# Keys scaled by one VectorE operation a head, probabilities scaled on GpSimd by a per-row scalar and in two portions

## The chip, the cores and the metric

The kernel runs on one core of one Trainium2 chip. The core has a matrix engine (TensorE, PE in the profile, with its weight loads listed apart as PEld), a vector engine (VectorE, DVE), an activation engine (ScalarE, ACT), a general engine (GpSimd, POOL) and a queue that issues transfers (SyncE, SP). Each engine takes its instructions in a fixed order and waits at an instruction until what it needs is there. The metric is the device time of one execution in microseconds (us); lower is better.

## What is computed

The reference is a trunk of two layers over 528 tokens (16 learned "meta" tokens ahead of 512 tokens) with 1024 channels. A layer normalises the stream, projects it, runs a causal pooling mixer and a latent attention side by side, gates both and adds the result to the stream. The change touches the attention alone, whose core is this:

```python
k = jnp.concatenate([k_nope, k_pe], axis=-1)      # 64 own columns a head, 32 rotary columns shared by all heads
q = rmsnorm(q, g_qn)
k = rmsnorm(k, g_kn)                              # one factor for each token and head
q = jnp.concatenate([q[..., :64], apply_rope(q[..., 64:], pos)], axis=-1)
k = jnp.concatenate([k[..., :64], apply_rope(k[..., 64:], pos)], axis=-1)
s = jnp.einsum('bqhd,bkhd->bhqk', q, k) * scale   # by blocks of 128 queries, causal
p = jax.nn.softmax(s, axis=-1)
o = jnp.einsum('bhqk,bkhd->bqhd', p, v)
```

There are 8 heads. The softmax divides each row of exponentials by its sum; the normalisation of the keys multiplies each key by a factor of its token and head.

## The kernel before

Channels lie on the 128 partitions and tokens along the free dimension. Each product in single precision is made of three matrix products (`mm3`, lines 187 to 193): a weight tile of 128 by 512 is loaded into `raw`, ScalarE rounds it to `whi` (line 183) and VectorE computes the rest `wlo = raw - whi` (line 184). Both inputs of that subtraction lie in SBUF. A stream of such products (`stream`, line 204) is the main work; the attention is threaded through it. In the program, `gap()` lets a set length of the stream run (2950 ns and 2700 ns a gap in layers 0 and 1, `FILL`), so that a head's parts stand between stretches of products. The order that each engine finally follows is set when the program is built: it is made with `schedule_with_timeline_sim=True`, so a scheduler lays the instructions out along a simulated timeline, and an instruction that stands later in the program may go ahead of one that is not ready there.

Heads go in pairs. The tile `kn[p]` holds the 64 own key rows of head 2p in partitions 0 to 63 and those of head 2p+1 in partitions 64 to 127. The tile `kp` holds the rotated shared key rows in both halves. For each head, `prep(h)` (line 842) builds the scaled keys `kf` (a buffer named `tmp`): VectorE multiplies the 64 own rows by the factors `bc` (line 849) and GpSimd multiplies the 64 shared rows by the same factors (line 850). `bc` is fetched two heads ahead by `spread_k` (line 838). Then `split` rounds `kf` to `kh` on ScalarE and takes the rest `kl` on VectorE (lines 297 and 298), the query of the head is split into `qhl`, and two transfers on the SP queue bring the rotary rows of the query (line 860).

`head(h)` (line 863) has two halves. In the first it computes the scores of query blocks 1 and 2 and part of block 3, takes the row minima on VectorE (`top`, line 879; it writes `bia`) and the exponentials of blocks 1 and 2 on ScalarE (`expo`, line 886, which also writes the row sums `rs`). A gap and the value products of the head before (`pv(prev, (0, 1))`) follow, and a second gap. In the second half come the rest of block 3, block 0 and their exponentials, the addition of the two partial sums of block 3 (line 918), one reciprocal of all four sums (line 919), and then GpSimd scales all four blocks. For each block it runs two multiplications of two tensors, one for the 16 meta columns, written to the pair's tile `pm` (line 924), and one for the other columns in place (line 926); in both the second tensor is the reciprocal spread along the row. The blocks `pt[0]` and `pt[1]` lie in `pa`, `pt[2]` and `pt[3]` in slots named `cq`. The number of columns is 144, 272, 400 and 528.

`pv` (line 929) of the next head transposes the scaled blocks on TensorE, splits the transposes (`th`, `tl`) and multiplies them with the values; for an odd head it splits `pm` (lines 939 to 941).

GpSimd also issues transfers that add weight tiles in memory for a later stage (`wsum`, `wsumgp`, line 353). Layer 1 has more vector work among the heads than layer 0: `mixed` (line 579) and the products made of seven instead of eight parts (`fast`, line 601, with lines 625 to 651).

Of the kernel before, what the change touches and what calls it, by code (L numbers as in the profile page):

```python
# [9 lines left out]
F32 = mybir.dt.float32  # L10
# [4 lines left out]
ALU = mybir.AluOpType  # L15
# [3 lines left out]
P = 128  # L19
# [3 lines left out]
NM = 16  # L23
# [49 lines left out]
def trunk(ctx, tc, xT, pos, win, wkr, wqb, wkb, wvb, wgr, wpu, wmu, wout, gains, const, yT):  # L73
    nc = tc.nc
    pe, act, dve, gp, sp = nc.tensor, nc.scalar, nc.vector, nc.gpsimd, nc.sync
# [11 lines left out]
    def nm(s):  # L87
        uid[0] += 1
        return f"{s}_{uid[0]}"
# [269 lines left out]
    class Layer:  # L359
# [158 lines left out]
        def k_factors(self):  # L518
            flat = lambda d: d.rearrange("h (s c) -> (h s) c", c=T // 16)
            na, ny, nt = (sm.tile([P, T // 16], F32, tag=t, name=nm(t)) for t in ("ka", "ky", "kt"))  # L520
            sp.dma_start(na, flat(ksr[self.l]))
            dve.tensor_scalar(na, na, 1.0 / QK, EPS, op0=ALU.mult, op1=ALU.add)
            newton(ny, na, nt)
            sp.dma_start(flat(kdr[self.l]), ny)
            self.bcs = {}
            for h in range(2):
                self.spread_k(h)

        def rope(self, out, src, a, b):
            n = b - a  # L530
# [307 lines left out]
        def spread_k(self, h):  # L838
            self.bcs[h] = bc = slot("bc", bufs=3)
            sp.dma_start(bc, kdr[self.l][h:h + 1, :].partition_broadcast(P))  # L840

        def prep(self, h):
            p, odd = h // 2, h % 2
            n0, r0 = (64, 0) if odd else (0, 64)
            kf = tmp()
            bc = self.bcs.pop(h)
            if h + 2 < H:
                self.spread_k(h + 2)
            dve.tensor_mul(kf[n0:n0 + 64, :], self.kn[p][n0:n0 + 64, :], bc[n0:n0 + 64, :])
            gp.tensor_mul(kf[r0:r0 + 64, :], self.kp[r0:r0 + 64, :], bc[r0:r0 + 64, :])  # L850
            kh, kl = slot("kh", F32R, bufs=2), slot("kl", F32R, bufs=2)
            split(kh, kl, kf[:, :T], 0, T)
            qh, ql = qhl[odd]
            x0 = self.x0
            src = self.qn[p][n0:n0 + 64, x0:T]
            act.activation(qh[n0:n0 + 64, x0:T], src, AF.Copy)
            dve.tensor_sub(ql[n0:n0 + 64, x0:T], src, qh[n0:n0 + 64, x0:T].bitcast(F32))
            g0 = 32 * (h % 4)
            for d, f in zip((qh, ql), self.qr[h // 4]):
                sp.dma_start(d[r0:r0 + 32, x0:T].bitcast(F32), f[g0:g0 + 32, x0:T].bitcast(F32))  # L860
            return kh, kl, qh, ql

        def head(self, h, kq, prev, between):
            kh, kl, qh, ql = kq
            odd = h % 2
# [19 lines left out]
            def expo(i, c, sv, pv):  # L885
                act.activation(pv, sv, AF.Exp, scale=-1.0, bias=bia[:, i:i + 1], accum_out=rs[:, c:c + 1])  # L886

            pt = [pa[:, 0:144], pa[:, 144:416], pb[:, 0:400], pc[:, 0:T]]
            sa = sct()
            s1, s3 = sa[:, 0:272], sa[:, 272:272 + SPL]  # L890
# [10 lines left out]
            top(2, 2, s2, causal(400))  # L901
            expo(1, 1, s1, pt[1])
            expo(2, 2, s2, pt[2])
            self.gap()
            between()
            self.pv(prev, (0, 1))
# [9 lines left out]
            expo(3, 3, s4, pt[3][:, SPL:T])  # L916
            expo(0, 0, s0, pt[0])
            dve.tensor_add(rs[:, 3:4], rs[:, 3:4], rs[:, 4:5])
            dve.reciprocal(rs[:, 0:4], rs[:, 0:4])  # L919
            if odd == 0:  # L920
                self.pm = sm.tile([P, 4, 32], F32, tag="pm", name=nm("pm"), bufs=2)
            for i in range(4):
                n = pt[i].shape[1]
                gp.tensor_mul(self.pm[:, i, 16 * odd:16 * odd + 16], pt[i][:, 0:NM],  # L924
                              rs[:, i:i + 1].to_broadcast([P, NM]))
                gp.tensor_mul(pt[i][:, NM:], pt[i][:, NM:], rs[:, i:i + 1].to_broadcast([P, n - NM]))  # L926
            return h, pt, self.pm

        def pv(self, prev, js):
# [483 lines left out]
```

## Time and profile before

| what | us |
|---|---|
| median of 3 runs | 786.03 |
| lowest and highest run | 784.74, 787.63 |
| the profiled execution | 788.06 |
| its span, from the first to the last instruction | 786.2 |

The difference between the profiled execution and its span, 1.86 us, is time outside the first and last instruction. The page of the profile gives for each engine its busy time and its share of the span. The views used below are: busy times by stretch of the span, waits (who waited for whom: total us, number of times, longest), groups of instructions by line (count, busy us, mean ns of one, then idle time just before them and who ended it), durations of one line (minimum/median/maximum), and the timeline. The heads of layer 0 lie between 160 and 340 us, those of layer 1 between 590 and 700 us.

### The profile page before, as it was taken

The numbers are of one execution on the slowest core, as the hardware profiler recorded it, in microseconds if no ns is written. First come the engines' busy times: TensorE is split into PE (matmuls) and PEld (weight loads), VectorE is DVE, ScalarE is ACT, GpSimd is POOL, SyncE is SP. The second block draws the span as 40 slices with busy tenths as digits, with TensorE's granted clock in tenths as the row PEclk, the third lists the DMA queues.
The fourth block names the chain that finished last, engine by engine and source line by source line (L and its number), as shares of the span: only waits on it lengthen the run. The fifth ranks groups of instructions, "written<-read, shape, count | busy, mean of one in ns | idle before, by whom it ended". The sixth has DMA issues, their size and how long they took to land.

```text
span 786.2 us, 15369 instructions
## 1 busy us (share of the span) xinstructions
PE 774.8 (99%) x5469; PEld 711.1 (90%) x5469; DVE 587.0 (75%) x1316; ACT 446.7 (57%) x1022; POOL 230.2 (29%) x319
## 2 busy tenths in 40 slices
PE   9999999999999999999999999999999999999998
PEld 8999899999999999999997898887788899788887
DVE  5848788547778977689764477775997899974984
ACT  8545655645556665545664356455667676654462
POOL 1024514203434342211320245131026235240213
PEclk9999999999999999999999999999999999999999
DMA  6242367765645465565653423435456566562655
GB/s 243 82 97 87 103 163 165 180 154 136 144 120 138 120 135 150 135 187 155 172 151 92 102 81 95 125 88 181 121 132 162 160 168 164 150 212 88 213 148 136
DMA packets 64909, 110.76 MB, mean 141 GB/s; under 512 B 10544, under 2 KB 16560, under 8 KB 64832
## 3 DMA queue, kind: packets, MB, share of 16 engines
q1 hardware_dynamic: 54928, 90.02, 38.4%
q0 software_dynamic: 8896, 17.92, 12.6%
q10 hardware_dynamic: 1008, 1.84, 0.6%
q8 instruction: 43, 0.70, 0.4%
q14 instruction: 34, 0.28, 0.1%
HBM read 100.18 MB, written 22.62 MB: 156 GB/s over the span
## 4 chain that ended last, share of the span: by engine, by line
PE 84%; DVE 6%; DMA 4%; issue 2%; ACT 2%; POOL 0%; SPq 0%; DVEq 0%; ACTq 0%
PE mm L188 24%; PE mm L192 23%; PE mm L191 23%; DVE wlo L184 2%; PE S L188 2%; PE S L191 2%; PE S L192 2%; PE mm L946 2%; DMA raw<-wsumgp 1%; DMA raw<-win 1%; PE o L952 1%; PE o L951 1%; PE S L500 1%; ACT whi L183 1%; DMA raw<-wqb 1%
## 5 line engine op out<-in xcount | busy, mean ns | idle before, releaser
L188 PE MATMUL mm<-hh,whi 128*128 128x264 f32 (+2 forms) x992 | 306.0, 311 | 1.6 <-DVE tmp L637 0.6
L192 PE MATMUL mm<-hh,wlo 128*128 128x264 f32 (+2 forms) x992 | 304.1, 309 | 1.1 <-DVE wlo L184 1.0
L191 PE MATMUL mm<-hl,whi 128*128 128x264 f32 (+2 forms) x992 | 304.5, 308 | 0.0
L184 DVE TENSOR_TENSOR wlo<-raw,whi 128x512 fp32r<-128x512 f32 (+2 forms) x261 | 191.9, 739 | 98.1 <-ACT whi L183 94.3
L183 ACT ACTIVATE whi<-raw 128x512 fp32r<-128x512 f32 (+2 forms) x261 | 156.5, 603 | 165.9 <-PE mm L191 91.0
L188 PEld LDWEIGHTS mm<-hh,whi 128*128 128x128 f32 x992 | 186.2, 188 | 12.9 <-issue 1.2
L192 PEld LDWEIGHTS mm<-hh,wlo 128*128 128x128 f32 x992 | 185.8, 188 | 10.6 <-DVE wlo L184 2.3
L191 PEld LDWEIGHTS mm<-hl,whi 128*128 128x128 f32 x992 | 186.8, 188 | 9.1
L188 PE MATMUL mm<-cq,whi 128*128 128x264 f32 (+2 forms) x140 | 44.2, 316 | 1.3 <-ACT racc L960 0.7
L192 PE MATMUL mm<-cq,wlo 128*128 128x264 f32 (+2 forms) x140 | 43.5, 313 | 0.6 <-DVE wlo L184 0.6
L191 PE MATMUL mm<-cq,whi 128*128 128x264 f32 (+2 forms) x140 | 43.5, 312 | 0.0
L879 DVE CUSTOM_DVE_ANT_0 S<-S,maskw,nqs 128x288 f32<-128x288 f32 (+4 forms) x80 | 38.4, 497 | 2.5 <-PE S L192 2.2
L702 POOL TENSOR_TENSOR racc<-racc,tmp 128x264 f32<-128x264 f32 (+1 forms) x15 | 14.3, 951 | 87.2 <-ACT tmp L701 87.1
L188 PE MATMUL mm<-u,whi 128*128 128x264 f32 (+1 forms) x108 | 35.3, 327 | 0.1
L192 PE MATMUL mm<-u,wlo 128*128 128x264 f32 (+1 forms) x108 | 34.8, 322 | 0.0
L298 DVE TENSOR_TENSOR tl<-mm,th 128x512 fp32r<-128x512 f32 (+1 forms) x64 | 29.2, 481 | 7.4 <-ACT th L297 6.3
L850 POOL TENSOR_TENSOR tmp<-kp,bc 64x528 f32<-64x528 f32 x16 | 25.6, 1602 | 30.5 <-issue 15.4
L353 POOL DMA_DIRECT2D wsum<-wout x8 | 6.9, 859 | 89.0 <-PE mm L192 73.0
L924 POOL TENSOR_TENSOR pm<-pa,rs 128x16 f32<-128x16 f32 x32 | 11.0, 345 | 72.6 <-DVE rs L919 66.7
L926 POOL TENSOR_TENSOR cq<-cq,rs 128x384 f32<-128x384 f32 (+1 forms) x32 | 32.2, 1005 | 0.0
L886 ACT ACTIVATE cq<-S,bia 128x400 f32<-128x400 f32 (+2 forms) x48 | 24.6, 515 | 12.2 <-DVE bia L914 7.2
L297 ACT ACTIVATE th<-mm 128x512 fp32r<-128x512 f32 (+1 forms) x64 | 25.9, 432 | 8.4 <-PE mm L946 7.3
(333 smaller groups left out, 1722.0 us busy)
## 6 DMA issues: line engine op xcount, KB each, us to landing
raw<-win SPq DMA_DIRECT2D x139, 256.0 KB, 3.0
raw<-wout SPq DMA_DIRECT2D x22, 256.0 KB, 3.5
bc<-kdr SPq DMA_DIRECT2D x16, 264.0 KB, 4.2
wsum<-wout SPq DMA_DIRECT2D x16, 256.0 KB, 3.5
raw<-wpu SPq DMA_DIRECT2D x16, 256.0 KB, 3.1
wsumgp<-win SPq DMA_DIRECT2D x16, 256.0 KB, 3.3
raw<-wmu SPq DMA_DIRECT2D x16, 256.0 KB, 2.7
raw<-wsumgp SPq DMA_DIRECT2D x16, 256.0 KB, 3.8
```

The costliest lines, as they stand in the source:

```text
L183: act.activation(hi[:, :n], raw[:, :n], AF.Copy)
L184: dve.tensor_sub(lo[:, :n], raw[:, :n], hi[:, :n].bitcast(F32))
L188: first = pe.matmul(out, wh, xh, start=start, stop=False, skip_group_check=more)
L191: pe.matmul(out, wh, xl, start=False, stop=False, skip_group_check=more)
L192: newest[0] = pe.matmul(out, wl, xh, start=False, stop=stop, skip_group_check=more)
L297: act.activation(hi[:, a:b], src, AF.Copy)
L298: dve.tensor_sub(lo[:, a:b], src, hi[:, a:b].bitcast(F32))
L850: gp.tensor_mul(kf[r0:r0 + 64, :], self.kp[r0:r0 + 64, :], bc[r0:r0 + 64, :])
L879: dve.tensor_tensor_reduce(out=sv, in0=sv, in1=mask, scale=nqs[:, i, h:h + 1], scalar=3e38, op0=ALU.add, op1=ALU.min, accum_out=bia[:, c:c ...
L886: act.activation(pv, sv, AF.Exp, scale=-1.0, bias=bia[:, i:i + 1], accum_out=rs[:, c:c + 1])
L926: gp.tensor_mul(pt[i][:, NM:], pt[i][:, NM:], rs[:, i:i + 1].to_broadcast([P, n - NM]))
L946: pe.transpose(tr[:, P * (i - j):P * (i - j + 1)], pt[i][:, NM + P * j:NM + P * (j + 1)], ident)
```

## The change

The keys: the shared rows in the lower half of `kp` are overwritten with the own rows of the pair's even head by a transfer on the SP queue (`lend`), so that `kp` holds a complete unscaled key of the even head, own rows below and shared rows above. The even head's `kf` is then one VectorE multiplication of 128 partitions. After the even head's multiplication is issued, another transfer writes the shared rows over the even head's rows in `kn[p]`, which makes `kn[p]` the complete key of the odd head, own rows above; its `kf` is again one VectorE multiplication. The first `lend` of a layer is issued in `k_factors`, the others in `prep` of the odd heads. GpSimd no longer takes part in the keys.

The probabilities: GpSimd scales each whole block in place by one `tensor_scalar`, whose factor is one number a partition, and copies the 16 scaled meta columns to `pm`. The blocks 1 and 2 get a reciprocal of their own right after their exponentials, in the first half of the head, and are scaled there; blocks 0 and 3 stay in the second half.

```diff
@@ k_factors
             for h in range(2):
                 self.spread_k(h)
+            self.lend(0)
...
+        def lend(self, p):
+            sp.dma_start(self.kp[0:64, :], self.kn[p][0:64, :])
+
         def prep(self, h):
...
-            dve.tensor_mul(kf[n0:n0 + 64, :], self.kn[p][n0:n0 + 64, :], bc[n0:n0 + 64, :])
-            gp.tensor_mul(kf[r0:r0 + 64, :], self.kp[r0:r0 + 64, :], bc[r0:r0 + 64, :])
+            dve.tensor_mul(kf, self.kn[p] if odd else self.kp, bc)
+            if not odd:
+                sp.dma_start(self.kn[p][0:64, :], self.kp[64:128, :])
+            elif p < 3:
+                self.lend(p + 1)
@@ head
+            if odd == 0:
+                self.pm = sm.tile([P, 4, 32], F32, tag="pm", name=nm("pm"), bufs=2)
+
+            def scale(blocks):
+                for i in blocks:
+                    gp.tensor_scalar(pt[i], pt[i], rs[:, i:i + 1], None, op0=ALU.mult)
+                    gp.tensor_copy(self.pm[:, i, 16 * odd:16 * odd + 16], pt[i][:, 0:NM])
...
             expo(1, 1, s1, pt[1])
             expo(2, 2, s2, pt[2])
+            dve.reciprocal(rs[:, 1:3], rs[:, 1:3])
+            scale((1, 2))
             self.gap()
...
             dve.tensor_add(rs[:, 3:4], rs[:, 3:4], rs[:, 4:5])
-            dve.reciprocal(rs[:, 0:4], rs[:, 0:4])
-            if odd == 0:
-                self.pm = sm.tile([P, 4, 32], F32, tag="pm", name=nm("pm"), bufs=2)
-            for i in range(4):
-                n = pt[i].shape[1]
-                gp.tensor_mul(self.pm[:, i, 16 * odd:16 * odd + 16], pt[i][:, 0:NM],
-                              rs[:, i:i + 1].to_broadcast([P, NM]))
-                gp.tensor_mul(pt[i][:, NM:], pt[i][:, NM:], rs[:, i:i + 1].to_broadcast([P, n - NM]))
+            dve.reciprocal(rs[:, 0:4:3], rs[:, 0:4:3])
+            scale((0, 3))
```

## The prediction

> **What bounds the kernel now.** I began with the page's busy times and its chain of waits, then cut the span into stretches at the two head stages.
>
> ```profile
> PE 774.8 (99%) x5469; PEld 711.1 (90%) x5469; DVE 587.0 (75%) x1316; ACT 446.7 (57%) x1022; POOL 230.2 (29%) x319
> ...
> PE 84%; DVE 6%; DMA 4%; issue 2%; ACT 2%; POOL 0%; SPq 0%; DVEq 0%; ACTq 0%
> ```
>
> ```profile
> core 0: us, PE busy (x) PEld busy (x) DVE busy (x) ACT busy (x) POOL busy (x), PEclk, DMA share, GB/s
> ...
> 160.00:340.00 180.00, 179.82 (x1463) 177.74 (x1463) 133.10 (x338) 102.08 (x264) 59.11 (x88) 1.00 0.57 137
> ...
> 590.00:700.00 110.00, 106.77 (x718) 96.75 (x717) 98.58 (x231) 75.19 (x197) 49.85 (x76) 1.00 0.63 170
> ```
>
> TensorE sets the end: it holds 84% of the chain and runs 774.8 of 786.2 us. The change gives it no work and takes none from it, so it can act only on the time in which TensorE stands still in the head stages, or add to it. In layer 0's heads (160 to 340) TensorE stands for 180 - 179.82 = 0.18 us: nothing is to be won there. In layer 1's heads (590 to 700) it stands for 110 - 106.77 = 3.23 us, and there VectorE is busy for 98.58 of 110 us, 90%, against 74% in layer 0's. So all that can be gained in the heads is 3.2 us, and VectorE is the engine that could lose it. The waits of that stretch, of TensorE, VectorE and ScalarE, say who is late:
>
> ```profile
> PE mm L192 <- DVE wlo L184: 1.0, 2, 0.8
> PE mm L188 <- ACT racc L960: 0.7, 1, 0.7
> PE mm L188 <- DVE tmp L637: 0.6, 1, 0.6
> PE o L951 <- DVE tmp L967: 0.6, 1, 0.6
> ```
>
> ```profile
> DVE wlo L184 <- ACT whi L183: 5.6, 7, 2.2
> DVE rs L918 <- ACT cq L886: 1.8, 3, 1.1
> ```
>
> ```profile
> ACT pmr L939 <- POOL pm L924: 4.3, 3, 2.2
> ```
>
> TensorE waits mostly for a VectorE result. VectorE itself waits 5.6 us for ScalarE's rounded weights, and ScalarE is held 4.3 us by GpSimd's `pm`. GpSimd is never waited for by TensorE but slows the two engines ahead of it. How, the timeline shows at one place, with the durations of the two VectorE lines beside it:
>
> ```profile
> 667.97 1.50 POOL L926 TENSOR_TENSOR cq<-cq,rs 128x512 f32<-128x512 f32 x1
> ...
> 669.55 1.99 POOL L850 TENSOR_TENSOR tmp<-kp,bc 64x528 f32<-64x528 f32 x1
> ```
>
> ```profile
> 668.50 1.52 DVE L184 TENSOR_TENSOR wlo<-raw,whi 128x512 fp32r<-128x512 f32 x1
> ...
> 670.28 1.80 DVE L184 TENSOR_TENSOR wlo<-raw,whi 128x512 fp32r<-128x512 f32 x1
> ```
>
> ```profile
> L184 DVE TENSOR_TENSOR wlo<-raw,whi x261: 281/692/1816, 6.4 to 773.9; 128x512 fp32r<-128x512 f32 x117, 128x256 fp32r<-128x256 f32 x10, 128x128 fp32r<-128x128 f32 x4
> ...
> L849 DVE TENSOR_TENSOR tmp<-kn,bc x16: 668/705/1756, 156.0 to 676.0; 64x528 f32<-64x528 f32 x16
> ```
>
> A subtraction of two SBUF tensors has a median of 692 ns, but 1.52 and 1.80 us where a GpSimd multiplication runs.
>
> **The change part by part.** These are the rows of VectorE and GpSimd in layer 1's heads:
>
> ```profile
> L184 DVE TENSOR_TENSOR wlo<-raw,whi 128x512 fp32r<-128x512 f32 x39 | 33.1, 849 | 5.6 <-ACT whi L183 5.6
> L849 DVE TENSOR_TENSOR tmp<-kn,bc 64x528 f32<-64x528 f32 x6 | 6.1, 1014 | 0.1
> ...
> L298 DVE TENSOR_TENSOR kl<-tmp,kh 128x528 fp32r<-128x528 f32 x6 | 4.2, 699 | 0.1
> ```
>
> ```profile
> L850 POOL TENSOR_TENSOR tmp<-kp,bc 64x528 f32<-64x528 f32 x6 | 10.2, 1698 | 20.4 <-issue 12.3 <-DVE rs L918 6.5 <-DVE kl L298 1.5
> L926 POOL TENSOR_TENSOR cq<-cq,rs 128x512 f32<-128x512 f32 x8 | 8.8, 1094 | 0.0
> L926 POOL TENSOR_TENSOR cq<-cq,rs 128x384 f32<-128x384 f32 x8 | 7.2, 900 | 0.0
> L924 POOL TENSOR_TENSOR pm<-cq,rs 128x16 f32<-128x16 f32 x16 | 6.1, 378 | 0.0
> L924 POOL TENSOR_TENSOR pm<-pa,rs 128x16 f32<-128x16 f32 x16 | 6.0, 372 | 31.5 <-DVE rs L919 29.6 <-DVE tl L298 1.8
> L926 POOL TENSOR_TENSOR pa<-pa,rs 128x256 f32<-128x256 f32 x8 | 5.5, 689 | 0.0
> L926 POOL TENSOR_TENSOR pa<-pa,rs 128x128 f32<-128x128 f32 x8 | 3.5, 440 | 0.0
> ```
>
> *Keys.* VectorE's operation grows from 64 to 128 partitions with the same 528 columns. Line 298 works on 128 by 528 in 699 ns and line 849 has a median of 705 ns on 64 by 528, so the wider operation costs the same: nothing added. GpSimd loses 1.70 us a head, and ScalarE's rounding of the keys loses one of its two releasers.
>
> *Probabilities.* GpSimd now spends 8.8 + 7.2 + 5.5 + 3.5 + 6.1 + 6.0 = 37.1 us, 4.64 us a head, and with the keys 6.34. The trace has no operation with a per-row factor on GpSimd. The nearest rows from both sides are a copy, with one input, and an addition of two full tensors:
>
> ```profile
> L476 POOL COPY tmp<-tmp x4: 398/772/806, 72.1 to 467.4; 32x264 f32<-32x264 f32 x4
> ```
>
> ```profile
> L702 POOL TENSOR_TENSOR racc<-racc,tmp 128x512 f32<-128x512 f32 x5 | 6.4, 1289 | 59.8 <-ACT tmp L701 59.8
> ```
>
> By its minimum the copy takes 398/264 = 1.51 ns a column with its fixed part, the addition 1289/512 = 2.52. The four blocks have 144 + 272 + 400 + 528 = 1344 columns: 2.0 us a head at the lower end, 3.4 at the upper. The four meta copies have the shape of line 924 (372 to 378 ns each in company): 1.5 us as an upper end, and 4 x 0.2 = 0.8 by estimate if they no longer meet as much of VectorE. I take 2.0 + 0.8 = 2.8 us a head, since an operation with one tensor is nearest to the copy; the ends are 2.8 and 4.9. Of 6.34 us that removes 56%, at the other end 23%.
>
> *What that gives VectorE.* In layer 1's heads the 39 subtractions cost 33.1 - 39 x 0.692 = 6.1 us more than at their median, line 849's six 6.1 - 6 x 0.705 = 1.9: 8.0 us lost to GpSimd. In proportion 56% is 4.5 us, 23% is 1.8. ScalarE gets back up to the 4.3 us before line 939, because GpSimd ends earlier. By the Trainium skill (SBUF — State Buffer, "SBUF: two separate sides") GpSimd and a VectorE operation with two SBUF inputs share one pair of ports as an exclusive lock, and the one that comes second is blocked for the whole of the other's instruction. The 1.80 us beside a GpSimd operation of 1.99 agree with it. By that rule fewer and shorter GpSimd operations count twice, and the relief would be nearer 1 - 0.44 x 0.44 = 81% of 8.0, 6.5 us; what this would make of the time is the second rival.
>
> *The added reciprocal.*
>
> ```profile
> L919 DVE RECIPROCAL rs<-rs x16: 160/178/178, 191.2 to 693.2; 128x4 f32<-128x4 f32 x16
> ```
>
> ```profile
> L886 ACT ACTIVATE cq<-S,bia x22: 441/494/597, 589.6 to 691.3; 128x288 f32<-128x288 f32 x8, 128x400 f32<-128x400 f32 x7, 128x240 f32<-128x240 f32 x7
> L886 ACT ACTIVATION_READ_ACCUMULATOR cq<-S,bia x22: 190/198/208, 590.0 to 691.6; 128x1 f32 x22
> ```
>
> One more a head, 8 x 0.17 = 1.4 us in layer 1's heads. It is also a new wait: it needs both exponentials of the first half, and behind it on VectorE stand the weight subtractions and the splits of transposes that TensorE waits for. At least this wait costs nothing, if other work is laid ahead of it for long enough; at most it lasts as long as both exponentials and their sums, 0.60 + 0.49 + 2 x 0.20 = 1.5 us a head, 12 us in the stage. The nearest row is the same kind of wait at line 918, 1.8 us in 8 heads; I take 1.8.
>
> *Transfers.* Per layer 4 `lend` and 4 back, on SP, of 64 x 528 x 4 bytes = 132 KB. The nearest rows are the query's transfers, also SBUF to SBUF, and what SP waits for between 550 and 700:
>
> ```profile
> qhl<-q SPq DMA_DIRECT2D x16, 66.0 KB, 2.9
> ```
>
> ```profile
> 658.50 1.16 SPq L860 DMA_DIRECT2D qhl<-q x2
> ```
>
> ```profile
> SPq L115 <- DVE wlo L184: 30.0, 19, 3.9
> ...
> SPq L840 <- POOL tmp L850: 2.8, 1, 2.8
> ```
>
> Each takes SP about 0.58 us to issue and some 3 to 4 us to land, and is needed a head later (110/8 = 14 us). Everything that it waits for was done a head earlier, so it holds up the weight loads behind it only by its issue, 8 x 0.58 = 4.6 us a stage, in a queue that waits 30.0 us for buffers anyway; the 2.8 us in which SP waited for line 850 go. I cost it at nothing. With that cover gone it would be 0.6 us a transfer on the way of a weight load, 4.6 us.
>
> *The sum in layer 1's heads.* VectorE: -4.5 + 1.4 + 1.8 = -1.3 us; ScalarE: up to -4.3 us of waiting. VectorE stays 88% busy, so some stalls remain; of TensorE's 3.23 us I give back half, 1.6, and nothing in layer 0's. Of the profiled execution's 788.06 us that leaves 786.5. It lies 2.03 us above the median of the runs, 786.03, so on their scale the forecast is **784.5 us**. Its own range is 783 to 786.
>
> **The rivals.** *The per-row factor is no cheaper* than a second tensor on GpSimd (4.9 us a head): VectorE gets 1.8 us and pays 1.4 + 1.8. Nothing changes, 786.0. For it: no row shows the operation. Against: the copy's 398 ns.
>
> *All the stalls go*: 786.03 - 3.2 = 782.8. For it: the 1.80 us beside 1.99 show a subtraction held for most of a GpSimd operation, so that shorter ones cost less than in proportion, and ScalarE's 4.3 us. The rule of the Trainium skill above speaks for it with its 6.5 us. Against: the chain through this stage also holds a late weight load, which no shorter operation mends:
>
> ```profile
> 660.38 4.96 DMA raw<-wsumgp
> ```
>
> *The new wait decides; slower.* Place: the reciprocal in the first half of a head of layer 1. VectorE's idle time there is 110 - 98.58 = 11.4 us, of which 5.6 is waiting for weights that can't be shifted; with the 4.5 gained and 1.4 spent, 8.9 us are free, 1.1 us a head. From there on each us of waiting is TensorE's. At 1.5 us a head it is (1.5 - 1.1) x 8 = 3.1 us: 789.1. If a rounding of weights (0.63 us in the row below) stands between the exponentials, 2.1 us a head and 8 us: 794. I take 790.5.
>
> ```profile
> L183 ACT ACTIVATE whi<-raw 128x512 fp32r<-128x512 f32 x40 | 25.2, 630 | 19.6 <-PE o L952 3.6 <-PE mm L946 3.5 <-PE mm L191 3.3
> ```
>
> For it: VectorE at 90%, and the changed lengths also let the planner lay out all engines anew, which can put this wait anywhere. Against: line 918 waits for the same thing and loses 1.8 us in 8 heads.
>
> **How the numbers follow.** Forecast 45%, no cheaper 15%, all stalls go 15%, slower 25%. About 0.5% (3.9 us) is what a measurement of this kernel can tell from no change: 782.1 to 790.0. Faster than that is a part of "all stalls go" and of luck in the layout, 12%. Slower is most of the slower case, 19%; the rest, 69%, is the same. The range goes from 781.8, all stalls and 1 us of spread between runs, to 790.8, the slower case with its lower half.
>
> **What would show it.** Right: GpSimd's time in layer 1's heads falls from 49.9 us to about 21; the mean of line 184 falls from 849 to below 770 ns; the wait of line 939 for GpSimd is gone; TensorE's 3.2 us of standing still shrink. Wrong: `tensor_scalar` rows above 2.5 ns a column; a wait of VectorE for line 886 in front of the new reciprocal of over 9 us in the stage; SP or a key split waiting for a `lend`; TensorE standing still in layer 0's heads, which would mean that the new layout, not the operations, decides.

## The result, and the profile after

The median of 7 runs of the changed kernel is **781.8 us** (780.91 to 783.88), against 786.03 before (now of 7 runs as well, with the same lowest, middle and highest): a ratio of 0.9951 with a 95% interval of 0.9939 to 0.9962, some 4.2 us or 0.5% less. The profiled execution took 781.06 us with a span of 779.3. The two profiled executions are 7.0 us apart, because the one of before lay 2.0 us above its median and this one 0.7 below; where a size matters, the medians decide.

The page of the changed kernel, busy times and the chain of waits by engine:

```profile
PE 772.7 (99%) x5469; PEld 711.3 (91%) x5469; DVE 570.4 (73%) x1332; ACT 445.9 (57%) x1022; POOL 232.1 (30%) x303
...
PE 90%; DMA 4%; DVE 3%; ACT 2%; issue 1%; POOL 1%; SPq 0%; ACTq 0%; DVEq 0%
```

TensorE runs the same 5469 matmuls and now holds 90% of the chain instead of 84%. Over the whole span it stood for 786.2 - 774.8 = 11.4 us before and stands for 779.3 - 772.7 = 6.6 now. GpSimd is *not* relieved: 232.1 us against 230.2, in 16 instructions fewer.

The stretches of the two head stages (busy us and instruction count of PE, PEld, DVE, ACT, POOL, then granted clock, DMA share, GB/s):

```profile
160.00:340.00 180.00, 180.00 (x1464) 177.90 (x1464) 126.66 (x347) 101.99 (x263) 58.93 (x80) 1.00 0.58 141
...
590.00:700.00 110.00, 109.55 (x736) 100.23 (x735) 92.06 (x240) 75.24 (x197) 54.95 (x69) 1.00 0.67 181
```

In layer 1's heads TensorE stands for 110 - 109.55 = 0.45 us instead of 3.23. VectorE is busy for 92.06 us instead of 98.58, although it has taken over GpSimd's key work; GpSimd is busy for 54.95 instead of 49.85.

VectorE's weight subtraction in that stretch (count, busy us, mean ns, then idle time before it and who ended it), and the new key operation in the whole run (minimum/median/maximum ns):

```profile
L184 DVE TENSOR_TENSOR wlo<-raw,whi 128x512 fp32r<-128x512 f32 x42 | 29.1, 695 | 10.0 <-ACT whi L183 9.5
```

```profile
L853 DVE TENSOR_TENSOR tmp<-kp,bc x8: 687/700/870, 155.0 to 662.8; 128x528 f32<-128x528 f32 x8
L853 DVE TENSOR_TENSOR tmp<-kn,bc x8: 689/698/703, 184.9 to 670.4; 128x528 f32<-128x528 f32 x8
```

The mean of line 184 has fallen from 849 to 695 ns, close to its median of before (692): hardly anything stretches it any more, and the longest one in this stretch takes 1.00 us instead of 1.80. The key operation over 128 partitions takes what the one over 64 took.

GpSimd in the same stretch, and below it the durations of its scaling in the whole run:

```profile
L900 POOL TENSOR_SCALAR cq<-cq,rs 128x528 f32<-128x528 f32 x8 | 14.9, 1864 | 0.0
L900 POOL TENSOR_SCALAR cq<-cq,rs 128x400 f32<-128x400 f32 x8 | 11.3, 1415 | 0.0
L900 POOL TENSOR_SCALAR pa<-pa,rs 128x144 f32<-128x144 f32 x8 | 8.2, 1023 | 9.5 <-DVE rs L936 5.1 <-ACT th L297 4.4
L900 POOL TENSOR_SCALAR pa<-pa,rs 128x272 f32<-128x272 f32 x7 | 8.1, 1161 | 28.9 <-DVE rs L919 28.9
L901 POOL COPY pm<-pa 128x16 f32<-128x16 f32 x16 | 6.4, 402 | 0.0
L901 POOL COPY pm<-cq 128x16 f32<-128x16 f32 x16 | 5.7, 359 | 0.0
```

```profile
L900 POOL TENSOR_SCALAR pa<-pa,rs x32: 632/960/2813, 180.7 to 689.4; 128x272 f32<-128x272 f32 x16, 128x144 f32<-128x144 f32 x16
L900 POOL TENSOR_SCALAR cq<-cq,rs x32: 1273/1597/2267, 181.7 to 690.3; 128x400 f32<-128x400 f32 x16, 128x528 f32<-128x528 f32 x16
```

A head's scaling (these six rows) takes 54.6/8 = 6.8 us of GpSimd, more than keys and probabilities together before (6.34). The shortest row, 632 ns for 144 columns, is 4.4 ns a column.

Waits between 580 and 700 us (total, times, longest):

```profile
DVE wlo L184 <- ACT whi L183: 10.5, 13, 2.3
...
ACT pmr L950 <- POOL pm L901: 0.4, 1, 0.4
```

ScalarE's 4.3 us of waiting for `pm` have become 0.4, and its waits for GpSimd's keys (1.6 us in two places before) are gone with that work. VectorE now waits 10.5 us for ScalarE's weights, not 5.6: it is ahead more of the time.

### The profile page after: what moved, and what is told of

The parts are those of the page before. It is cut to its first block, busy times and chain, and to the rows that moved or that the text cites. A ratio compares the mean times of both kernels' runs of the same rounds, so it can differ in the third digit from the quotient of the medians.

```text
span 779.3 us, 15360 instructions
## 1 busy us (share of the span) xinstructions
PE 772.7 (99%) x5469; PEld 711.3 (91%) x5469; DVE 570.4 (73%) x1332; ACT 445.9 (57%) x1022; POOL 232.1 (30%) x303
## 4 chain that ended last, share of the span: by engine, by line
PE 90%; DMA 4%; DVE 3%; ACT 2%; issue 1%; POOL 1%; SPq 0%; ACTq 0%; DVEq 0%
PE mm L188 26%; PE mm L192 25%; PE mm L191 25%; DMA raw<-win 2%; PE S L191 2%; PE S L192 2%; PE S L188 2%; PE mm L957 2%; PE o L963 1%; PE o L962 1%; PE S L500 1%; DVE wlo L184 1%; ACT whi L183 1%; DMA raw<-wqb 1%; PE mm L402 1%
## 5 line engine op out<-in xcount | busy, mean ns | idle before, releaser
L184 DVE TENSOR_TENSOR wlo<-raw,whi 128x512 fp32r<-128x512 f32 (+2 forms) x261 | 182.5, 703 | 104.6 <-ACT whi L183 100.5
L900 POOL TENSOR_SCALAR pa<-pa,rs 128x272 f32<-128x272 f32 (+1 forms) x32 | 33.2, 1036 | 103.3 <-DVE rs L919 63.9
L900 POOL TENSOR_SCALAR cq<-cq,rs 128x400 f32<-128x400 f32 (+1 forms) x32 | 51.1, 1597 | 0.0
L886 DVE CUSTOM_DVE_ANT_0 S<-S,maskw,nqs 128x272 f32<-128x272 f32 (+4 forms) x80 | 38.6, 498 | 5.3 <-PE S L192 5.0
L297 ACT ACTIVATE th<-mm 128x512 fp32r<-128x512 f32 (+1 forms) x64 | 26.2, 433 | 10.3 <-PE mm L957 9.8
L191 PE MATMUL mm<-kn,whi 128*128 128x264 f32 (+1 forms) x96 | 30.6, 320 | 0.0
```

What stands on the lines that cost most here:

```text
L184: dve.tensor_sub(lo[:, :n], raw[:, :n], hi[:, :n].bitcast(F32))
L191: pe.matmul(out, wh, xl, start=False, stop=False, skip_group_check=more)
L297: act.activation(hi[:, a:b], src, AF.Copy)
L886: dve.tensor_tensor_reduce(out=sv, in0=sv, in1=mask, scale=nqs[:, i, h:h + 1], scalar=3e38, op0=ALU.add, op1=ALU.min, accum_out=bia[:, c:c ...
L900: gp.tensor_scalar(pt[i], pt[i], rs[:, i:i + 1], None, op0=ALU.mult)
```

## The experiments

Two theories of where the 4.2 us come from. **Contention**: VectorE runs shorter, since fewer GpSimd instructions read two tensors. **Waiting**: what ScalarE and TensorE need no longer stands in GpSimd's queue. The change has three parts: *keys* (two transfers a pair, one VectorE multiplication a head), *form* (one `tensor_scalar` and a copy in place of two multiplications a block) and *move* (blocks 1 and 2 and their reciprocal in the first half). All eight combinations were timed, then single costs. Each time of a variant is the median of 8 to 12 runs, each ratio is against the kernel before on the same chip (785.82 to 786.35 us), with an interval of about 1 us on either side, so that two variants differ clearly from some 1.5 us on.

| version | median us | ratio (95%) | L184 mean ns, 590 to 700 | TensorE standing there, us | GpSimd busy there, us |
|---|---|---|---|---|---|
| before | 786.03 | 1 | 849 | 3.23 | 49.85 |
| keys | 784.18 | 0.9982 (0.9970 to 0.9994) | 778 | 1.71 | 43.03 |
| form | 788.52 | 1.0033 (1.0019 to 1.0047) | 727 | 1.55 | 58.90 |
| move | 789.27 | 1.0038 (1.0022 to 1.0053) | 811 | 4.62 | 50.62 |
| keys, form | 783.31 | 0.9974 (0.9963 to 0.9985) | 707 | 0.95 | 56.33 |
| keys, move | 784.37 | 0.9982 (0.9970 to 0.9994) | 762 | 1.26 | 40.62 |
| form, move | 786.31 | 0.9998 (0.9990 to 1.0007) | 780 | 2.01 | 64.76 |
| keys, form, move | 781.80 | 0.9951 (0.9939 to 0.9962) | 695 | 0.45 | 54.95 |

### One part alone

**keys_alone**, the kernel before with

```diff
+            self.lend(0)
...
+        def lend(self, p):
+            sp.dma_start(self.kp[0:64, :], self.kn[p][0:64, :])
...
-            dve.tensor_mul(kf[n0:n0 + 64, :], self.kn[p][n0:n0 + 64, :], bc[n0:n0 + 64, :])
-            gp.tensor_mul(kf[r0:r0 + 64, :], self.kp[r0:r0 + 64, :], bc[r0:r0 + 64, :])
+            dve.tensor_mul(kf, self.kn[p] if odd else self.kp, bc)
+            if not odd:
+                sp.dma_start(self.kn[p][0:64, :], self.kp[64:128, :])
+            elif p < 3:
+                self.lend(p + 1)
```

> Only the keys change (one VectorE multiplication of 128 partitions, the transfers between kp and kn); the scaling of the probabilities is that of before. Contention (GpSimd operations with two SBUF inputs hold VectorE operations with two SBUF inputs): the longest meetings, those with line 850, are gone, those with the scaling stay; the mean of the weight subtraction in layer 1's heads falls from 849 to about 760 ns, time 783 to 784.5. Waiting (what counted is that the split of the keys and pm no longer wait for GpSimd): most of the gain, 782 to 783, also with a mean of 800 ns or more. Layout (the planner's new order decides): anything from 782 to 788, and not the sum with the other parts.

Measured 784.18 us, 1.8 less: the time that contention had given, slower than waiting's. VectorE's subtraction gets half-way to its undisturbed length:

```profile
L184 DVE TENSOR_TENSOR wlo<-raw,whi 128x512 fp32r<-128x512 f32 x41 | 31.8, 778 | 5.0 <-ACT whi L183 4.8
```

**form_alone**, all four blocks still in the second half:

```diff
+            def scale(blocks):
+                for i in blocks:
+                    gp.tensor_scalar(pt[i], pt[i], rs[:, i:i + 1], None, op0=ALU.mult)
+                    gp.tensor_copy(self.pm[:, i, 16 * odd:16 * odd + 16], pt[i][:, 0:NM])
...
-            for i in range(4):
...
-                gp.tensor_mul(pt[i][:, NM:], pt[i][:, NM:], rs[:, i:i + 1].to_broadcast([P, n - NM]))
+            scale((0, 1, 2, 3))
```

> Only the form of the scaling changes (tensor_scalar on the whole block and a copy of 16 columns, all four blocks in the second half); keys as before. Contention: GpSimd is busy longer (about 6.6 instead of 4.6 us a head) and yet VectorE is held less, since these read one tensor: mean of the weight subtraction in layer 1's heads 849 to about 790 ns, time 784.5 to 785.5. Waiting: GpSimd ends each head 2 us later, the keys and pm behind it are later, so slower than before: 787 to 789. Layout: anything from 782 to 788.

Measured 788.52 us: 2.5 **slower**, as waiting had it, with line 184 down to 727 ns, further than contention had it. A faster VectorE did not make a faster kernel. The timeline of GpSimd at the end of the last head (start us, us) shows one place where the form is late, here in form_alone, then in the changed kernel:

```profile
701.19 2.86 POOL L893 TENSOR_SCALAR cq<-cq,rs 128x400 f32<-128x400 f32 x2
...
704.46 0.33 POOL L894 COPY pm<-cq 128x16 f32<-128x16 f32 x2
```

```profile
690.27 1.60 POOL L900 TENSOR_SCALAR cq<-cq,rs 128x528 f32<-128x528 f32 x1
...
691.95 0.19 POOL L901 COPY pm<-cq 128x16 f32<-128x16 f32 x1
```

The dearer scaling, all behind the last exponential, is done at 704.8 us; in the kernel before it was done at 698.7 and in the changed one at 692.1. After it TensorE stands:

```profile
700.00:740.00 40.00, 38.50 (x178) 31.05 (x177) 23.70 (x41) 16.86 (x34) 7.59 (x12) 1.00 0.42 125
```

That stretch of form_alone has 1.5 us of standing, against 0.06 both before and in the changed kernel (39.94 of 40 us busy). TensorE waits there for ScalarE (0.8 us for line 1036, 0.7 for the rounding of a transpose); that ScalarE was late because of the scaling is argued, not shown. And it explains a part only: the profiled execution of form_alone, 787.55 us, lay below that of the kernel before, 788.06, so one execution of each cannot account for a difference of 2.5 us between medians.

**move_alone**, with the old two multiplications a block in `scale`:

```diff
+            dve.reciprocal(rs[:, 1:3], rs[:, 1:3])
+            scale((1, 2))
...
-            dve.reciprocal(rs[:, 0:4], rs[:, 0:4])
+            dve.reciprocal(rs[:, 0:4:3], rs[:, 0:4:3])
+            scale((0, 3))
```

> Only the place changes: blocks 1 and 2 get their own reciprocal and are scaled in the first half, with the two multiplications of two tensors of before; keys as before. Contention: the meetings are as many and as long, the mean of the weight subtraction stays within 820 to 880 ns, one more reciprocal a head: 785.5 to 787. Waiting: pm and the keys are ready about 2 us earlier in a head: 783.5 to 785. Layout: anything from 782 to 788.

Measured 789.27 us, 3.3 slower than before on the same chip and outside all three forecasts. In the heads of layer 1 TensorE stands for 4.62 us, 4.1 of them waiting for results of VectorE (1.8 for `wlo`). The new reciprocal does not show as the cause: VectorE's wait for the exponentials in front of it is 0.9 us in two places. Why the move alone costs time stays open.

### Two parts

**keys_and_form** is the changed kernel with

```diff
-            dve.reciprocal(rs[:, 1:3], rs[:, 1:3])
-            scale((1, 2))
...
-            dve.reciprocal(rs[:, 0:4:3], rs[:, 0:4:3])
-            scale((0, 3))
+            dve.reciprocal(rs[:, 0:4], rs[:, 0:4])
+            scale((0, 1, 2, 3))
```

> The whole change but for the place: all four blocks are scaled in the second half. Contention: no GpSimd operation with two tensors is left in the heads, mean of the weight subtraction in layer 1's heads about 700 ns, time as after, 781.3 to 782.8. Waiting: pm comes 2 us later than after, 783 to 785. Layout: anything from 781 to 788.

**keys_and_move** is the changed kernel with

```diff
-                    gp.tensor_scalar(pt[i], pt[i], rs[:, i:i + 1], None, op0=ALU.mult)
-                    gp.tensor_copy(self.pm[:, i, 16 * odd:16 * odd + 16], pt[i][:, 0:NM])
+                    n = pt[i].shape[1]
+                    gp.tensor_mul(self.pm[:, i, 16 * odd:16 * odd + 16], pt[i][:, 0:NM],
+                                  rs[:, i:i + 1].to_broadcast([P, NM]))
+                    gp.tensor_mul(pt[i][:, NM:], pt[i][:, NM:], rs[:, i:i + 1].to_broadcast([P, n - NM]))
```

> The whole change but for the form: blocks 1 and 2 are scaled in the first half, with the two multiplications of two tensors of before. Contention: VectorE is held by the scaling as with the keys alone (mean of the weight subtraction in layer 1's heads 760 to 800 ns against 695 after), and one more reciprocal a head: 784 to 785.5, no faster than the keys alone (784.2). Lateness of the scaling (what counts is when GpSimd has the blocks ready): with the short multiplications and the split place they are ready earliest of all, so at least as fast as after: 781 to 782.3.

**form_and_move** is the changed kernel without both transfers and with

```diff
-            dve.tensor_mul(kf, self.kn[p] if odd else self.kp, bc)
+            dve.tensor_mul(kf[n0:n0 + 64, :], self.kn[p][n0:n0 + 64, :], bc[n0:n0 + 64, :])
+            gp.tensor_mul(kf[r0:r0 + 64, :], self.kp[r0:r0 + 64, :], bc[r0:r0 + 64, :])
```

> The whole change but for the keys, which GpSimd still multiplies (line 850). Contention: VectorE is held by line 850 alone (mean of the weight subtraction in layer 1's heads 720 to 740 ns), and the late end of the scaling after the last head, which the form alone showed (GpSimd until 704.8 us instead of 698.7), is gone: 784 to 786. Lateness: about 782 to 783.5, since the keys wait for GpSimd 1.7 us a head at most. Layout: anything up to 789.

Measured 783.31, 784.37 and 786.31 us. The first is waiting's time, with a mean of line 184 (707 ns) that is contention's; the second has the time and the mean (762 ns) of contention; the third, with a mean of 780 ns, is slower than both theories had it and within the layout's range only. Putting one part on top of the others, as differences to the kernel before on the same chip:

| part added | to before | to one other part | to both others |
|---|---|---|---|
| keys | -1.8 | -5.2 (to form), -4.7 (to move) | -4.7 |
| form | +2.5 | -0.9 (to keys), -2.8 (to move) | -2.8 |
| move | +3.3 | +0.4 (to keys), -2.0 (to form) | -1.5 |

The keys gain in every company. Form and move both cost when alone. On top of both other parts they gain 2.8 and 1.5 us; on top of the keys alone neither differs clearly from nothing. The parts don't add up: 1.8 - 2.5 - 3.3 would be 4.0 us lost, and 4.2 were won. Line 184's mean doesn't order the times either: form_alone has 727 ns and 788.5 us, keys_and_move 762 ns and 784.4. But it nearly orders TensorE's standing in the stage: with the eight versions in order of the mean, only two neighbouring pairs are swapped there. So VectorE's hold is seen in the stage, and the time has more in it than the stage.

### Is it the keys' place in GpSimd's queue, or VectorE's hold?

**keys_through_one** puts GpSimd back into the keys' path, but with an instruction that reads one tensor. It is the changed kernel with a multiplication by 1.0 in place:

```diff
             dve.tensor_mul(kf, self.kn[p] if odd else self.kp, bc)
+            gp.tensor_scalar(kf[r0:r0 + 64, :], kf[r0:r0 + 64, :], 1.0, None, op0=ALU.mult)
```

> The changed kernel with GpSimd back in the way of the keys, but with one tensor: after VectorE's multiplication GpSimd multiplies 64 rows of the key by the number 1, in place (estimate 1.6 us a head, the length of line 850), and the split waits for it, behind the scaling on GpSimd's queue. Contention: one input does not hold VectorE; mean of the weight subtraction in layer 1's heads 695 to 715 ns, time 781.5 to 783.5. Waiting (what moving the keys gained was that they no longer stand in GpSimd's queue): back to the changed kernel with the old keys, 785.5 to 787.

Measured 786.66 us (ratio 1.0007, 0.9995 to 1.0020): all of the gain is gone, as waiting had it, and it stands where form_and_move stands, 786.31, whose GpSimd instruction in the same path reads two tensors. Line 184's mean is 738 ns here and 780 there, so VectorE's hold differs and the time doesn't. GpSimd's added operation has a mean of 1.74 us, about that of the one which the change removed:

```profile
L854 POOL TENSOR_SCALAR tmp<-tmp 64x528 f32<-64x528 f32 x6 | 10.5, 1742 | 8.8 <-DVE tmp L853 5.0 <-ACT whi L183 2.1 <-ACT tmp L651 1.5
```

The timelines of VectorE, GpSimd, ScalarE and TensorE where TensorE stands longest follow one key through the engines (start us, us; in brackets the idle time before and who ended it):

```profile
589.23 0.70 DVE L853 TENSOR_TENSOR tmp<-kp,bc 128x528 f32<-128x528 f32 x1
```

```profile
589.66 1.42 POOL L901 TENSOR_SCALAR cq<-cq,rs 128x400 f32<-128x400 f32 x1
591.04 0.19 POOL L902 COPY pm<-pa 128x16 f32<-128x16 f32 x1
591.32 1.96 POOL L854 TENSOR_SCALAR tmp<-tmp 64x528 f32<-64x528 f32 x1
```

```profile
593.52 0.49 ACT L894 ACTIVATE pa<-S,bia 128x272 f32<-128x272 f32 x1 [0.29 <-DVE bia L887]
...
594.00 0.63 ACT L297 ACTIVATE kh<-tmp 128x528 fp32r<-128x528 f32 x1
```

```profile
594.69 0.39 PE L188 MATMUL S<-kh,qhl 128*128 128x272 f32 x1 [2.71 <-ACT kh L297]
```

VectorE has the key ready at 589.23 + 0.70 = 589.93 us. GpSimd takes it up at 591.32, behind a scaling and a copy of another head, and is done at 593.28, 3.35 us after VectorE. By then one more exponential is laid ahead of its rounding on ScalarE, and TensorE, which has waited 2.71 us for the rounded key, starts the scores at 594.69.

In layer 1's eight heads the rounding of a key begins 2.0 to 4.6 us after VectorE's multiplication here, 0.2 to 1.7 us after it in the changed kernel. So GpSimd in the path of the keys costs as much as the whole change gains, while most of VectorE's hold stays lifted (738 ns against 849 before and 695 in the changed kernel): contention alone doesn't explain the keys' gain.

Three things limit this. The added operation always stands behind VectorE's, which is harder than the kernel before: there GpSimd's rows of a key were done ahead of VectorE's in five of layer 1's eight heads, and 1.2 to 5.5 us after them in three. Second, it isn't shown that the kernel before lost its time in this way: in its stage ScalarE stood only 1.6 us for GpSimd's keys and no wait of TensorE for a rounded key is listed; TensorE's waits, shown with the prediction, were mostly for results of VectorE. Third, the equal times of keys_through_one and form_and_move have different causes: after its long stall the first runs at a lower clock (last section). Its mean granted clock is 0.995 to 0.998 in 11 of 12 executions; in all 12 of form_and_move it is 0.999 or 1.0.

**idle_two_inputs** and **idle_one_input** load GpSimd behind the keys with three small operations a head, whose result nothing reads. In the changed kernel, after the keys' multiplication, with `ghost` of 128 by 176 elements:

```diff
+            for c0 in (0, 176, 352):
+                gp.tensor_mul(ghost[64:128, :], kf[64:128, c0:c0 + 176], bc[64:128, c0:c0 + 176])
```

> The changed kernel with idle work on GpSimd that can't go ahead: behind VectorE's multiplication of the keys, three multiplications of that key by bc, 64 rows by 176 columns (1.7 us a head), into a tile that nobody reads. Contention: they meet VectorE where line 850 did; mean of the weight subtraction in layer 1's heads 735 to 780 ns, time 783 to 785.5. Waiting: nobody waits for them, but the scaling behind them is later: 782 to 784, mean near 700.

```diff
+            for c0 in (0, 176, 352):
+                gp.tensor_scalar(ghost[64:128, :], kf[64:128, c0:c0 + 176], gn[64:128, 0:1], None, op0=ALU.mult)
```

> The same idle work at the same place with one tensor (three tensor_scalar by a number a row, 2.2 us a head). Contention: mean of the weight subtraction 690 to 710 ns, 781.5 to 783, below the kernel with two inputs by 1.5 us or more. Waiting: GpSimd is busy longer, so as slow as the kernel with two inputs or slower.

Measured 785.09 us with two tensors (0.9987, 0.9975 to 0.9999) and 787.32 with one (1.0018, 1.0003 to 1.0033): the one that should free VectorE is the slower, in the order that waiting had given. The first time is contention's, though, and above waiting's. GpSimd's ghosts between 590 and 700 us, two inputs first:

```profile
L856 POOL TENSOR_TENSOR ghost<-tmp,bc 64x176 f32<-64x176 f32 x18 | 11.8, 658 | 6.2 <-DVE tmp L854 2.5 <-DVE rs L939 2.5
```

```profile
L856 POOL TENSOR_SCALAR ghost<-tmp,gn 64x176 f32<-64x176 f32 x18 | 17.5, 971 | 5.7 <-DVE rs L939 2.5 <-DVE tmp L854 1.8
```

Line 184's counterpart has almost the same mean in both (719 and 714 ns, where contention had 735 to 780 and 690 to 710), so the pair hardly changed the hold. What differs is 17.5 - 11.8 = 5.7 us of GpSimd time, and with it ScalarE's wait for `pm` (0.2 and 1.5 us) and one wait of VectorE of 1.0 us for the keys' buffer that a ghost still read. These two traces don't stand for the medians: that of the first took 787.12 us, 2.0 above its median, that of the second 785.74, the shortest of its twelve. A lower clock has a part here too: 7 executions of the second had a mean clock of 0.998, none of the first one below 0.999. What the medians show is that idle time on GpSimd behind the keys takes back most of the gain or all of it, and that the instruction with fewer inputs is not the cheaper.

**ghost_two_inputs** and **ghost_one_input** were the first form of this pair, with operands that don't depend on the key multiplication, laid after the transfers:

```diff
+            for c0 in (0, 176, 352):
+                gp.tensor_mul(ghost[64:128, :], self.kp[64:128, c0:c0 + 176], bc[64:128, c0:c0 + 176])
```

> The changed kernel with idle work added on GpSimd: at the place where line 850 stood, for each head three multiplications of kp and bc, 64 rows by 176 columns each, into a tile that nobody reads (about 1.7 us a head). Nothing waits for their result; bc comes free after them. Contention: they hold VectorE as line 850 did: mean of the weight subtraction in layer 1's heads back to 740 to 780 ns, time 783 to 785, some half of what was won. Lateness or layout: nobody waits, so 781 to 782.6 with the mean near 700.

```diff
+            for c0 in (0, 176, 352):
+                gp.tensor_scalar(ghost[64:128, :], bc[64:128, c0:c0 + 176], gn[64:128, 0:1], None, op0=ALU.mult)
```

> The same idle work with one tensor as input: three tensor_scalar of bc by a number a row, 64 rows by 176 columns, longer on GpSimd than the other (about 2.1 us a head). Contention: one input does not hold VectorE: mean of the weight subtraction near 700 ns, time 781 to 783, and below the kernel with two inputs. If it is GpSimd's time that counts, whatever its inputs: as slow as the kernel with two inputs or slower, 783 to 785.

Measured 787.07 us, above both forecasts, and 783.30, just above contention's. The pair doesn't tell the theories apart: only 11 and 9 of the layer's 24 ghosts lay in the stretch, and GpSimd stood for most of 10.3 and 6.3 us in front of them, waiting for transfers of `bc`, with the scaling queued behind (two inputs first):

```profile
L860 POOL TENSOR_TENSOR ghost<-kp,bc 64x176 f32<-64x176 f32 x11 | 7.6, 693 | 10.3 <-DMA bc<-kdr 9.8
```

```profile
L860 POOL TENSOR_SCALAR ghost<-bc,gn 64x176 f32<-64x176 f32 x9 | 7.8, 870 | 6.3 <-DMA bc<-kdr 5.8
```

Line 184's mean came out at 719 and 704 ns, far from the slowdown that contention by two tensors was to bring. Taken alone the pair would have spoken for contention; the idle pair, placed among the scaling, came out the other way.

### The disputed cost by itself

**pairs** is a kernel that leaves out the whole computation: it repeats single GpSimd and VectorE operations of 128 by 512 elements, each alone and then at the same time.

```diff
+    phase((8, lambda: gp.tensor_add(ao, a1, a2)),
+          (12, lambda: dve.tensor_sub(xo, x1, x2)))
+    phase((8, lambda: gp.tensor_mul(ao, a1, rs.to_broadcast([P, 512]))),
+          (12, lambda: dve.tensor_sub(xo, x1, x2)))
+    phase((8, lambda: gp.tensor_scalar(ao, a1, rs, None, op0=ALU.mult)),
+          (12, lambda: dve.tensor_sub(xo, x1, x2)))
+    phase((8, lambda: gp.tensor_copy(ao, a1)),
+          (12, lambda: dve.tensor_sub(xo, x1, x2)))
```

> Leaves out the whole computation: only GpSimd and VectorE operations on tiles of 128 by 512 in phases, each form alone and in pairs, so its time is no time of the kernel. Alone: GpSimd addition of two tensors 1290 ns, a tensor times a spread number 1030, tensor_scalar by a number a row 1550, copy 600 to 700; VectorE's subtraction 690 from SBUF, 690 with one input from PSUM. In pairs, contention by inputs: VectorE's subtraction from SBUF rises to 1000 ns or more beside the two GpSimd forms with two tensors and stays below 760 beside tensor_scalar and copy; with an input from PSUM it stays at 690 beside all. Contention whatever the inputs (an exclusive hold for the whole instruction): beside tensor_scalar it rises as well, to over 1000.

In each pair twelve subtractions of VectorE meet eight GpSimd instructions, and in some phases the last of them run alone. So VectorE's durations are given as minimum/median/maximum, beside two full tensors (L110), a tensor and a spread column (L112), a copy (L116) and `tensor_scalar` (L114):

```profile
L110 DVE TENSOR_TENSOR xo<-x,x x12: 691/1632/1635, 39.1 to 54.6; 128x512 f32<-128x512 f32 x12
```

```profile
L112 DVE TENSOR_TENSOR xo<-x,x x12: 691/1409/1411, 55.4 to 69.1; 128x512 f32<-128x512 f32 x12
```

```profile
L116 DVE TENSOR_TENSOR xo<-x,x x12: 692/979/981, 84.5 to 94.8; 128x512 f32<-128x512 f32 x12
```

```profile
L114 DVE TENSOR_TENSOR xo<-x,x x12: 691/876/1061, 69.9 to 79.7; 128x512 f32<-128x512 f32 x12
```

Groups (count, busy us, mean ns) with one operand in PSUM, beside two tensors (L118) and `tensor_scalar` (L120), and from SBUF alone (L107):

```profile
L118 DVE TENSOR_TENSOR yo<-ps,x 128x512 f32<-128x512 f32 x12 | 8.3, 691 | 0.5
L120 DVE TENSOR_TENSOR yo<-ps,x 128x512 f32<-128x512 f32 x12 | 8.3, 691 | 2.4 <-POOL ao L117 2.1
L107 DVE TENSOR_TENSOR xo<-x,x 128x512 f32<-128x512 f32 x6 | 4.2, 693 | 24.1 <-POOL ao L106 24.0
```

GpSimd's own groups when alone, `tensor_scalar`, two tensors, a tensor and a spread column, copy:

```profile
L105 POOL TENSOR_SCALAR ao<-a,rs 128x512 f32<-128x512 f32 x5 | 7.8, 1562 | 0.5
...
L103 POOL TENSOR_TENSOR ao<-a,a 128x512 f32<-128x512 f32 x5 | 6.3, 1261 | 6.3 <-DVE ps L92 6.0
L104 POOL TENSOR_TENSOR ao<-a,rs 128x512 f32<-128x512 f32 x5 | 5.2, 1038 | 0.4
L106 POOL COPY ao<-a 128x512 f32<-128x512 f32 x5 | 3.1, 613 | 0.3
```

Contention is real: 693 ns become 1632 beside two tensors and 1409 beside the form that the kernel had. Beside a copy they become 979, and beside `tensor_scalar`, whose instructions are longer, the median lies half-way between 691 and 1061: by the mean of 876, half of the subtractions are held. Both are more than the 760 that I had set as the most. A GpSimd instruction that reads one tensor costs VectorE 0.29 us (copy, 613 ns alone) or 0.37 us (`tensor_scalar`, 1562 ns alone), one that reads two 0.72 us (1038 ns alone) or 0.94 us (1261 ns alone). GpSimd is held as well: in company its instructions take 1602 ns (two tensors), 1389 (spread column), 976 (copy) and 1726 (`tensor_scalar`). And the per-row factor is the dearest of the four forms on GpSimd: 1562 ns against 1038 for the one that it replaces.

## Why the prediction was right, and where not

**TensorE sets the end; its standing still in layer 1's heads is the prize.** Right, within limits. It fell from 3.23 to 0.45 us. That is not all of the gain: over the whole span TensorE stands 11.4 - 6.6 = 4.8 us less, and its busy time is 774.8 - 772.7 = 2.1 us shorter with the same matmuls; together the 6.9 us between the spans. Why busy time shrinks no run here shows. The ends of matmuls are modelled, so waits of the weight loads may lie in it; those for VectorE's `wlo` fell from 3.4 to 0.7 us.

**Keys at no cost for VectorE.** Right: 698 to 700 ns against 705. That this one edit would gain in every company the prediction didn't say; it counted the keys as 1.70 of the 3.5 us a head that GpSimd would be spared. All four comparisons give them 1.8 to 5.2 us.

**GpSimd's scaling, 2.8 us a head with ends of 2.8 and 4.9.** Wrong in sign: GpSimd's time in the stage was to fall from 49.9 us to about 21 and rose to 54.95. The scaling takes 6.8 us a head; even the shortest of three blocks, 632 ns (144 columns), 1273 (400) and about 1600 (528), make 3.5 us and pass the 3.4 us that the upper end had for all four. An operation by a per-row factor was put nearest to a copy because it reads one tensor. The row "above 2.5 ns a column", named as what would show the step wrong, came: 632/144 = 4.4 and 1273/400 = 3.2. So the condition of the rival *no cheaper* was met, and its time, 786.0, was not.

**VectorE's 8.0 us lost to GpSimd, 4.5 won back in proportion to GpSimd's time.** The proportion was wrong, and that rescued the sum by luck: GpSimd got longer, and VectorE was relieved all the same. By pairs the hold of one instruction goes first by how many tensors GpSimd reads: `tensor_scalar` is the longest of the four forms and holds VectorE about as little as the copy. The mean of 695 ns on line 184 says that nearly all of its 6.1 us came back. The Trainium skill (SBUF — State Buffer, "SBUF: two separate sides") has the shared ports locked for the whole of an instruction, for a GpSimd instruction that reads at all. For two tensors the trace of pairs is near it, 1632 ns beside instructions of 1602 in company; beside `tensor_scalar`, 1726 ns in company, subtractions of 691 and 1061 ns do not agree.

**The new reciprocal, 1.4 us and 1.8 of waiting.** The wait was overrated: 0.9 us in the whole run. Below, the waits of VectorE in the changed kernel for the exponentials:

```profile
DVE rs L919 <- ACT cq L893: 0.9, 2, 0.8
```

So the rival in which this wait decides did not come about. Nor does this wait explain that the move alone is 3.3 us slower: it is 0.9 us there too, and the cause was not found.

**Transfers at nothing.** The cost was right as far as the runs show, the reason wrong: SP did wait for a `lend` before the transfer back, which the prediction had named as a sign of being wrong,

```profile
SPq L855 <- DMA kp<-kn: 26.3, 8, 4.7
```

26.3 us in eight places, all eight transfers back. So what it waits for was not done a head earlier: the order laid out by the scheduler puts the two transfers close together, and SP stands until the first has landed. That SP had this time to spare is seen in keys_alone, which waits 23.8 us in the same eight places and is faster than before.

**The sum, half of 3.23 us.** This is the mis-sized term. 784.5 was forecast, 781.8 measured: outside the forecast's own 783 to 786, on the lower edge of the whole range, and among the times below 782.1 that had been given 12%. The direction was right. TensorE got back 2.78 of the 3.23 us in the stage, not 1.6, and some 2 us of standing elsewhere, half of them behind 700 us, for which the sum had no term. Between medians 4.2 us went, where 1.6 were given. (The 88% for VectorE counted 1.8 us of waiting as work; without it the sum gives 87%, and 84% was measured.)

The time is a little below the rival *all the stalls go* (782.8), and its mechanism, VectorE's hold gone nearly in full, did occur. How much of the gain it carries stays open. For it speaks that TensorE's standing in the stage follows the hold in the eight versions. Against it as the whole cause speak form_alone, with less hold and a longer time, and keys_through_one, which loses all the gain with GpSimd back in the path of the keys, though behind VectorE there and not beside it. What is shown is that the keys' part gains in every company; whether by the wait that it removes or by the hold, the runs don't separate.

## What to carry to other kernels

Before work is shifted to make an engine shorter, look at who reads its queue and how late: here the change won time though GpSimd's total grew; what had gone was its 1.7 us a head ahead of the scores. The slower form on the same engine cost 2.5 us alone and gained 2.8 on top of the other two parts. Parts that share one laid-out order don't add up: time every combination before one of them is credited. A mean that improves on a busy engine, 849 to 727 ns, is no forecast of the end, not even of its sign.

## What the runs showed of the hardware that was not expected

GpSimd's multiplication by a per-row factor takes 1562 ns for 512 columns and a copy of them 613, though both read one tensor. And a short stall of TensorE can cost more than itself. In keys_through_one the 2.71 us before 594.69 are followed by a lower granted clock (the third number from the end of a row):

```profile
590.00:600.00 10.00, 7.29 (x36) 6.08 (x35) 5.64 (x19) 4.88 (x15) 9.82 (x11) 0.83 0.73 167
```

In ghost_two_inputs a stall of 1.93 us does it; the stretches, and TensorE's timeline:

```profile
610.00:615.00 5.00, 3.07 (x24) 2.67 (x23) 4.30 (x8) 4.62 (x11) 4.22 (x7) 1.00 0.35 98
615.00:620.00 5.00, 5.00 (x29) 4.89 (x28) 1.88 (x5) 1.68 (x4) 2.89 (x4) 0.66 0.72 199
```

```profile
614.20 0.35 PE L189 MATMUL mm<-hh,whi 128*128 128x256 f32 x1 [1.93 <-DVE tl L299]
614.39 0.28 PE L192 MATMUL mm<-hl,whi 128*128 128x256 f32 x1
614.50 0.28 PE L193 MATMUL mm<-hh,wlo 128*128 128x256 f32 x1
...
617.09 0.41 PE L192 MATMUL mm<-cq,whi 128*128 128x256 f32 x1
617.30 0.41 PE L193 MATMUL mm<-cq,wlo 128*128 128x256 f32 x1
```

Matmuls of one shape start every 0.11 us right after the stall and every 0.21 us from about 615 to 618.4, half the pace, which by estimate is 3.4 x (0.21 - 0.11)/0.21 = 1.6 us lost on top of 1.93. The Trainium skill (TensorE: Matmul & The Clock Gate, "Why this matters for your kernels") warns of gaps above some 3 us; here less than 2 us was enough, in a stretch in which TensorE had stood for 5 - 3.07 = 1.93 us. In idle_one_input it is the same after 1.97 us of standing in 5 us, the longest piece 1.66: the next 5 us have a clock of 0.66. In the other ten traces of the kernel no 5 us between 5 and 775 have more than 1.35 us of standing, and the clock is 1.00 in all of them. By the estimate, a stall like that of ghost_two_inputs costs 3.5 us in all, where the change gained 4.2.
